# Gate projections by seven products: sums of weights formed a group ahead, in blocks of their own, and the first two gates by plain products

## The chip, the cores and the metric

One core of one Trainium2 chip. The metric is the device time of one execution in microseconds (us): the kernel before took 1498.84 us in the median of 3 runs (1498.33 to 1502.33).

## What is computed

One layer of a hybrid attention block on x of 256 rows by 2048 columns, in fp32, with 256 rows of memory:

```python
proj = rms_norm(x, g_mix) @ w_in          # heads' q, k, v and, last, 3 x 2048 gate columns
o_fox, o_sb, o_mem = ...                  # forgetting, stick-breaking and memory attention
g = sigmoid(gates.reshape(b, s, 3, 2048) + b_gate)
merged = g[..., 0, :] * (o_fox @ w_br_fox) + g[..., 1, :] * (o_sb @ w_br_sb) + g[..., 2, :] * (o_mem @ w_br_mem)
x = x + merged @ w_out
u = causal_depthwise_conv(rms_norm(x, g_ffn) @ w_up, conv_w, conv_b)
x = x + (silu(u_gate) * u_val) @ w_down
```

The change is in the gate columns of `proj`: six pieces of 1024 columns, for m = 0, 1 (the halves of the 2048 columns) and b = 0, 1, 2 (the three branches). They are called gate (m, b) here.

## The kernel before

**Splitting.** Each fp32 product is made of three faster ones. A weight tile `raw` is copied to a rounded high half `hi` by ScalarE (L141, or L278 in `parts`), and VectorE subtracts to get the low half `lo` (L142, L279). `three` (L282) issues x_hi w_hi, x_lo w_hi and x_hi w_lo, L284 to L286. There are four raw buffers of 1024 columns (`WBUFS`) and four each of `hi` and `lo` (`SBUFS`), used in turn: a split waits until TensorE is done with the piece four back.

**Old products.** `product` (L156) makes 512 columns for both halves of the rows (t = 0, 1) in two PSUM banks, from pieces of two k-tiles by 512 columns, 12 matmuls of 512 columns each, with a tick() after each piece. `proj` (L701) is `product` on `w_in`.

**Blocked products.** `blocked` (L322) makes 1024 columns by a plan, a string of groups, each for one pair of k-tiles. In a group "e" (`eight`, L342) there are 8 block products, 24 matmuls, with a tick after each 12. In a group "s" there are 7, 21 matmuls, as in Strassen's scheme: `seven_here` (L389) loads the pair's two raw tiles, forms four sums of weight blocks in place in them with four VectorE instructions (L397, L398, L401, L402), and splits them again (`hi_t`, `lo_t`, on L278 and L279). Products of sums go to four more banks Y (the name yg in the profile; the plain ones are xg). After the last "s" the generator `gathered` (L951) combines the Y banks with eight VectorE instructions and one copy, and when the gate is done four instructions on L982 add the X banks, scaled by `rstd`. `blocked` ends with finish(). PSUM has eight banks: X takes four, Y four, and before the first "s" the other four go to attention heads.

**Order of the work.** Matmuls of `three` stand in TensorE's queue in the order of the program from the gate stage on (`ordered[0]`). Small work is written as generators: `later()` queues one, `tick()` (L102) advances up to two of them (`WINDOW`) and the background ones, and `finish()` (L123) runs all that is queued to its end, with no gate matmul between. Other instructions are ordered by a scheduler by priority, within their dependencies.

**Heads.** `sb_head` (L864) is such a generator, for six stick-breaking heads, two at a time: scores z (L871, L872), exponentials and logarithms on ScalarE, masks on GpSimd (L859), suffix sums r (L888, L890) from `ls` (L883, L884), then `weighted` (L712) with L716 and L717 for the output. Heads 0 and 1 end and heads 2 and 3 run during gate (0,0); heads 4 and 5 begin in it and end in its finish().

**Preloads.** `weight_sums` (L243) is a background generator: from the first products on it loads halves of rows of w_out and w_down for later "s" groups, sums them with three VectorE instructions (L265 to L267) and stores the sums to DRAM (L270). It starts one half every 4 ticks, and every 8 ticks once `"heads"` has been issued (L983).

**Gate loop.** L942 to L986: plans in `g_plans` (L226), biases on L949, sigmoids on L985. After the gates of one m come the branch products and the merge; `merged_T` (L916) transposes the merged rows, for m = 0 during gate (1,0).

Of the kernel before, what the change touches and what calls it, by code (L numbers as in the profile page):

```python
# [11 lines left out]
AF = mybir.ActivationFunctionType  # L12
ALU = mybir.AluOpType
# [4 lines left out]
NT = S // P  # L18
D = 2048
# [12 lines left out]
C_GATE = C_MQ + MEM_W  # L32
PIECE = 1024
# [8 lines left out]
def hybrid_block(  # L42
# [25 lines left out]
    nc = tc.nc  # L68
# [12 lines left out]
    def bank(name):  # L81
        return pp.tile([P, 512], F32, tag="bank", name=name)
# [34 lines left out]
    issued = set()  # L117
# [5 lines left out]
    def finish():  # L123
        while waiting or active:
            tick(beside=False)
# [97 lines left out]


    o_plans = ("eessesse", "eesesese")
    g_plans = (("eeeeeeee", "esesesee", "esesesee"), ("eesessee", "esesesee", "esesesee"))  # L226
    d_plans = ("ef" * 5 + "ssef" * 4 + "seeee", "efefefesssfe" + "ssse" * 2 + "ssssee")
    T1, T3, T4, T2 = range(4)
    FS2, FS4, FS3, FS1 = range(4)
    in_order = tc.keep_in_program_order  # L230
# [43 lines left out]
    def parts(src, name):  # L274
        n = src.shape[1]
        hi = wp.tile([P, PIECE], F32R, tag="hi", bufs=SBUFS, name=f"hi_{name}")
        lo = wp.tile([P, PIECE], F32R, tag="lo", bufs=SBUFS, name=f"lo_{name}")
        nc.scalar.copy(hi[:, :n], src)  # L278
        nc.vector.tensor_tensor(lo[:, :n], src, hi[:, :n].bitcast(F32), ALU.subtract)  # L279
        return [(hi[:, i : i + 512], lo[:, i : i + 512]) for i in range(0, n, 512)]  # L280
# [41 lines left out]
    def blocked(name, w, nb, n0, plan, pair, sums, raw_tile, t4_tile, gathered, ready=None, form=None, apart=None):  # L322

        wv = by_k(w)
        X = [[bank(f"x{name}{nb}_{t}_{n}") for n in range(2)] for t in range(NT)]
        Y = []
        ns = plan.count("s")

        def a_of(p, j, t):
            v = pair(p, j)  # L330
            return v[:, t * P : (t + 1) * P], v[:, S + t * P : S + (t + 1) * P]

        def f_of(p, f):
            v = sums(p, f)
            return v[:, 0], v[:, 1]

        def load(k):
            raw = raw_tile(f"raw_{name}{nb}_{k}")
            nc.sync.dma_start(raw, wv[:, k, n0 : n0 + PIECE])
            return raw  # L340

        def eight(p, first, last):  # L342
            by_bank = last and apart is not None
            w = []
            for j in range(2):
                w.append(parts(load(2 * p + j), f"{name}{nb}_{2 * p + j}"))
                if not by_bank:
                    for t in range(NT):
                        for n in range(2):
                            three(X[t][n], *a_of(p, j, t), w[j][n], first and j == 0, last and j == 1)  # L350
                tick()
            if by_bank:
                for t in range(NT):
                    for n in range(2):
                        m = 256 if (t, n) == (1, 1) else 512
                        for j in range(2):
                            wj = [part[:, :m] for part in w[j][n]]
                            three(X[t][n][:, :m], *a_of(p, j, t), wj, last=j == 1)
                        if m < 512:
                            apart.append(bank("apart")[:, m:])  # L360
                            for j in range(2):
                                wj = [part[:, m:] for part in w[j][n]]
                                three(apart[0], *a_of(p, j, t), wj, j == 0, j == 1)

        def seven(p, first, last):
            kept = sums_of[name, nb, p]
            raw0 = raw_tile(f"raw_{name}{nb}_{2 * p}")
            nc.sync.dma_start(raw0[:, :512], wv[:, 2 * p, n0 : n0 + 512])
            nc.sync.dma_start(raw0[:, 512:], kept[:, T3])
# [12 lines left out]
            T1w, T2w = parts(raw2, f"t_{name}{nb}_{p}")  # L382
            three(Y[2], *f_of(p, FS1), T1w, first, last)
            three(Y[1], *f_of(p, FS2), T2w, first, last)
            (T4w,) = parts(raw3, f"t4_{name}{nb}_{p}")
            three(X[1][0], *a_of(p, 1, 1), T4w)
            tick()

        def seven_here(p, first, last):  # L389
            raw0, raw1 = load(2 * p), load(2 * p + 1)  # L390
            (B00,) = parts(raw0[:, :512], f"{name}{nb}_{2 * p}")
            three(Y[0], *a_of(p, 0, 0), B00, first, last)
            B10, B11 = parts(raw1, f"{name}{nb}_{2 * p + 1}")
            three(X[0][0], *a_of(p, 1, 0), B10)
            three(X[0][1], *f_of(p, FS4), B11)
            b0, b1 = (raw.rearrange("p (n c) -> p n c", n=2) for raw in (raw0, raw1))
            nc.vector.tensor_tensor(b0[:, 0], b0[:, 0], b0[:, 1], ALU.add)  # L397
            nc.vector.tensor_tensor(b0[:, 1], b0[:, 1], b1[:, 1], ALU.add)  # L398
# [3 lines left out]
            nc.vector.tensor_tensor(b1[:, 0], b1[:, 0], b1[:, 1], ALU.add)  # L402
# [7 lines left out]
        by_seven = seven if t4_tile else seven_here  # L410
# [145 lines left out]
    def block(name, dt=F32):  # L556
        return bp.tile([P, 1024], dt, tag="blk", name=name)
# [4 lines left out]
    def rows_of(b):  # L562
        return b.rearrange("p (t n) -> p t n", t=NT)
# [377 lines left out]
    for m in range(2):  # L941
        gate = []  # L942
        for b, plan in enumerate(g_plans[m]):
            g, bias = [], []

            def biases(m=m, b=b, bias=bias):
                for n in (2 * m, 2 * m + 1):
                    bias.append(gp.tile([P, 512], F32, tag="bg", name=f"bg_{n}_{b}"))
                    nc.sync.dma_start(bias[-1], b_gate[0, b, n * 512 : (n + 1) * 512].partition_broadcast(P))  # L949
# [21 lines left out]
            if "s" not in plan:  # L971
                biases()
            X = blocked(
                "g", w_in, f"{m}{b}", C_GATE + b * D + m * PIECE, plan, lambda p, j: xT(2 * p + j),
                lambda p, f: xs[:, p, f], raw_g, None, gathered, biases,
            )
            for n in range(2):
                if "s" not in plan:
                    g.append(rows_of(block(f"g_{m}_{b}_{n}")))
                for t in range(NT):  # L980
                    add = g[n][:, t] if "s" in plan else bias[n]
                    nc.vector.scalar_tensor_tensor(g[n][:, t], X[t][n], rstd[:, t : t + 1], add, ALU.mult, ALU.add)  # L982
            issued.add("heads")  # L983
            for n in range(2):
                sigmoid = nc.scalar.activation(g[n], g[n], AF.Sigmoid)  # L985
                if (m, b) == (0, 0):  # L986
                    in_order(sigmoid)
            gate.append(g)
        if m == 1:
            later(merged_sums())  # L990
        for n in range(2):
# [236 lines left out]
```

## Time and profile before

| | us |
|---|---|
| median of 3 runs | 1498.84 |
| the profiled execution's own time | 1498.03 |
| its span | 1496.3 |
| TensorE busy | 1470.8 |
| VectorE busy | 1211.8 |
| ScalarE busy | 843.1 |

PE is TensorE's matmuls, PEld its weight loads, DVE is VectorE, ACT ScalarE, POOL GpSimd, SP the queue that issues DMAs. A group's row reads: line, engine, operation, written<-read by the program's names without numbers, shapes, xcount, then busy us and mean ns of one, then the idle time of that engine just before and what ended it. A row of the waits reads: who waited <- for whom: us in total, times, longest. A row of the timeline reads: start, length, engine, line, what, and in brackets the idle time before and its releaser. The gates' matmuls run from 311.56 to 361.58 us (gate (0,0)), from 374.60 to 462.4 (gates (0,1) and (0,2)) and from 508.16 to 647.7 (m = 1); branch products lie between and behind.

### The profile page before, as it was taken

The numbers are of one execution on the slowest core, as the hardware profiler recorded it, in microseconds if no ns is written. First come the engines' busy times: TensorE is split into PE (matmuls) and PEld (weight loads), VectorE is DVE, ScalarE is ACT, GpSimd is POOL, SyncE is SP. The second block draws the span as 40 slices with busy tenths as digits, with TensorE's granted clock in tenths as the row PEclk, the third lists the DMA queues.
The fourth block names the chain that finished last, engine by engine and source line by source line (L and its number), as shares of the span: only waits on it lengthen the run. The fifth ranks groups of instructions, "written<-read, shape, count | busy, mean of one in ns | idle before, by whom it ended". The sixth has DMA issues, their size and how long they took to land.

```text
span 1496.3 us, 20704 instructions
## 1 busy us (share of the span) xinstructions
PE 1470.8 (98%) x7328; PEld 1232.8 (82%) x7328; DVE 1211.8 (81%) x1844; ACT 843.1 (56%) x1201; POOL 18.3 (1%) x46
## 2 busy tenths in 40 slices
PE   9999999998999999999999999999999999999999
PEld 7888888886877876788888888888888888888887
DVE  5777677876898898998887988887787777998877
ACT  6754454464554445545657665655565565675664
POOL 0000000021000000000000000000000000000000
PEclk9999999998999999999999999999999999999999
DMA  9697798786678677697867888887666666798896
GB/s 315 199 299 228 236 298 255 223 259 221 201 234 270 212 230 236 217 315 245 285 206 242 293 277 281 292 283 241 191 187 197 185 183 203 237 322 270 259 329 222
DMA packets 201430, 369.42 MB, mean 247 GB/s; under 512 B 13530, under 2 KB 82030, under 8 KB 201070
## 3 DMA queue, kind: packets, MB, share of 16 engines
q1 hardware_dynamic: 199998, 365.99, 76.4%
q10 hardware_dynamic: 1328, 2.11, 0.4%
q8 instruction: 57, 0.93, 0.3%
q14 instruction: 47, 0.39, 0.1%
HBM read 335.54 MB, written 32.51 MB: 246 GB/s over the span
## 4 chain that ended last, share of the span: by engine, by line
PE 83%; DVE 8%; DMA 5%; issue 2%; ACT 2%; POOL 0%; SPq 0%; ACTq 0%; DVEq 0%; POOLq 0%
PE u L1131 22%; PE u L1132 11%; PE xd L284 4%; PE xd L286 4%; PE xd L285 4%; DMA raw_g<-in_w_in_dram 2%; PE f L284 2%; PE f L286 2%; PE f L285 2%; PE b L286 2%; PE xg L286 2%; PE xg L284 2%; PE xg L285 2%; PE b L284 2%; PE b L285 2%
## 5 line engine op out<-in xcount | busy, mean ns | idle before, releaser
L1131 PE MATMUL u<-hT,hi_u 128*128 128x512 f32 x1232 | 428.5, 394 | 0.0
L1132 PE MATMUL u<-hT,lo_u 128*128 128x256 f32 x1232 | 341.4, 277 | 0.0
L142 DVE TENSOR_TENSOR lo_u<-raw_u,hi_u 128x1024 fp32r<-128x1024 f32 x176 | 215.0, 1222 | 83.2 <-ACT hi_u L141 82.5
L1131 PEld LDWEIGHTS u<-hT,hi_u 128*128 128x128 f32 x1232 | 231.0, 187 | 53.4
L141 ACT CAST hi_u<-raw_u 128x1024 fp32r<-128x1024 f32 x176 | 184.7, 1050 | 136.7 <-PE u L1131 117.4
L1132 PEld LDWEIGHTS u<-hT,lo_u 128*128 128x128 f32 x1232 | 231.4, 188 | 0.0
L278 ACT CAST hi_g<-raw_g 128x1024 fp32r<-128x1024 f32 (+1 forms) x96 | 92.7, 982 | 75.4 <-DMA raw_g<-in_w_in_dram 45.9
L279 DVE TENSOR_TENSOR lo_d<-raw_d,hi_d 128x1024 fp32r<-128x1024 f32 x88 | 106.7, 1222 | 20.5 <-ACT hi_d L278 17.8
L278 ACT CAST hi_d<-raw_d 128x1024 fp32r<-128x1024 f32 x88 | 92.0, 1054 | 47.8 <-PE xd L285 22.1
L279 DVE TENSOR_TENSOR lo_g<-raw_g,hi_g 128x1024 fp32r<-128x1024 f32 (+1 forms) x96 | 108.2, 1139 | 12.5 <-ACT hi_g L278 12.2
L286 PE MATMUL xg<-lo_g,xT 128*128 128x512 f32 x231 | 90.4, 391 | 1.1 <-DVE lo_g L279 1.1
L284 PE MATMUL xg<-hi_g,xT 128*128 128x512 f32 x231 | 90.9, 394 | 0.0
L285 PE MATMUL xg<-hi_g,xT 128*128 128x512 f32 x231 | 90.0, 390 | 0.0
L141 ACT CAST hi_f<-raw_f 128x1024 fp32r<-128x1024 f32 (+1 forms) x40 | 38.6, 968 | 51.7 <-PE f L285 43.1
L284 PE MATMUL xd<-hi_d,aT 128*128 128x512 f32 x170 | 66.1, 389 | 0.0
L285 PE MATMUL xd<-hi_d,aT 128*128 128x512 f32 x170 | 66.1, 389 | 0.0
L286 PE MATMUL xd<-lo_d,aT 128*128 128x512 f32 x170 | 66.1, 389 | 0.0
L1131 PE MATMUL u<-hT_rest,hi_u 128*128 128x512 f32 x176 | 62.1, 393 | 0.0
L141 ACT CAST hi_s<-raw_s 128x1024 fp32r<-128x1024 f32 (+1 forms) x40 | 38.4, 961 | 40.9 <-PE s L285 25.7
L1103 ACT ACTIVATE y<-u,taps 128x256 f32<-128x256 f32 x88 | 49.2, 595 | 14.7 <-DVE u L1100 14.7
L142 DVE TENSOR_TENSOR lo_f<-raw_f,hi_f 128x1024 fp32r<-128x1024 f32 (+1 forms) x40 | 44.4, 1117 | 15.2 <-ACT hi_f L141 13.5
L142 DVE TENSOR_TENSOR lo_s<-raw_s,hi_s 128x1024 fp32r<-128x1024 f32 (+1 forms) x40 | 44.4, 1115 | 14.8 <-ACT hi_s L141 14.4
(467 smaller groups left out, 3323.2 us busy)
## 6 DMA issues: line engine op xcount, KB each, us to landing
raw_u<-in_w_up_dram SPq DMA_DIRECT2D x176, 512.0 KB, 4.6
raw_g<-in_w_in_dram SPq DMA_DIRECT2D x96, 512.0 KB, 4.4
raw_d<-in_w_down_dram SPq DMA_DIRECT2D x66, 512.0 KB, 5.3
pre_d<-in_w_down_dram SPq DMA_DIRECT2D x88, 256.0 KB, 4.7
kept_d<-pre_d SPq DMA_DIRECT2D x44, 512.0 KB, 5.9
raw_f<-in_w_in_dram SPq DMA_DIRECT2D x32, 512.0 KB, 5.0
raw_s<-in_w_in_dram SPq DMA_DIRECT2D x32, 512.0 KB, 5.3
raw_o<-in_w_out_dram SPq DMA_DIRECT2D x25, 512.0 KB, 5.4
```

The costliest lines, as they stand in the source:

```text
L141: pin(nc.scalar.copy(hi[:, :m], raw[:, :m]))
L142: pin(nc.vector.tensor_tensor(lo[:, :m], raw[:, :m], hi[:, :m].bitcast(F32), ALU.subtract))
L278: nc.scalar.copy(hi[:, :n], src)
L279: nc.vector.tensor_tensor(lo[:, :n], src, hi[:, :n].bitcast(F32), ALU.subtract)
L284: fix(nc.tensor.matmul(o, lhsT=ah, rhs=w[0], start=first, stop=False))
L285: fix(nc.tensor.matmul(o, lhsT=al, rhs=w[0], start=False, stop=False))
L286: fix(nc.tensor.matmul(o, lhsT=ah, rhs=w[1], start=False, stop=last))
L1103: nc.scalar.activation(y, u[:, 2:], AF.Identity, scale=tap(2), bias=tap(3))
L1131: nc.tensor.matmul(ps[i], lhsT=hi[:, j, c], rhs=hT(k + j), start=first, stop=False)
L1132: nc.tensor.matmul(ps[i][:, :S], lhsT=lo[:, j, c], rhs=hT(k + j)[:, :S], start=False, stop=last)
```

## The change

Gates (0,0) and (0,1) get empty plans: they are made by `proj` in two halves each, and their sums are scaled with the bias added. The plan of gate (1,0) becomes that of the others. So 12 groups by seven are left of 15. In the gates' groups "s" the sums go to two tiles of the pool `block`, `t13` and `t42` (t0_g and t1_g in the program's names); a new function `prepared` issues the loads and the sums directly after the group before has been issued. `ready`, which loads the biases, now also calls finish(), sets `"heads"` and applies the sigmoid of gates (0,0) and (0,1) when it is first called, at the first "s" of gate (0,2); and it is called before the Y banks are taken.

```diff
-    g_plans = (("eeeeeeee", "esesesee", "esesesee"), ("eesessee", "esesesee", "esesesee"))
+    g_plans = (("", "", "esesesee"), ("esesesee", "esesesee", "esesesee"))
...
+        def prepared(p):
+            raw0, raw1 = load(2 * p), load(2 * p + 1)
+            t13, t42 = (t4_tile(f"t{i}_{name}{nb}_{p}") for i in range(2))
+            b0, b1, u, v = (w.rearrange("p (n c) -> p n c", n=2) for w in (raw0, raw1, t13, t42))
+            nc.vector.tensor_tensor(u[:, 0], b0[:, 0], b0[:, 1], ALU.add)
+            nc.vector.tensor_tensor(u[:, 1], b0[:, 1], b1[:, 1], ALU.add)
+            nc.vector.tensor_tensor(v[:, 1], u[:, 0], b1[:, 1], ALU.add)
+            nc.vector.tensor_tensor(v[:, 0], v[:, 1], b1[:, 0], ALU.add)
+            return raw0, raw1, t13, t42
...
         def seven_here(p, first, last):
-            raw0, raw1 = load(2 * p), load(2 * p + 1)
+            raw0, raw1, t13, t42 = ahead.pop(p)
...
-            b0, b1 = (raw.rearrange("p (n c) -> p n c", n=2) for raw in (raw0, raw1))
-            nc.vector.tensor_tensor(b0[:, 0], b0[:, 0], b0[:, 1], ALU.add)
-            nc.vector.tensor_tensor(b0[:, 1], b0[:, 1], b1[:, 1], ALU.add)
             tick()
-            T1w, T3w = parts(raw0, f"t_{name}{nb}_{2 * p}")
-            nc.vector.tensor_tensor(b1[:, 1], b1[:, 1], b0[:, 0], ALU.add)
-            nc.vector.tensor_tensor(b1[:, 0], b1[:, 0], b1[:, 1], ALU.add)
+            T1w, T3w = parts(t13, f"t_{name}{nb}_{2 * p}")
...
-            T4w, T2w = parts(raw1, f"t_{name}{nb}_{2 * p + 1}")
+            T4w, T2w = parts(t42, f"t_{name}{nb}_{2 * p + 1}")
...
                 if s == 0:
+                    if ready:
+                        ready()
                     Y += [bank(f"y{name}{nb}_{j}") for j in range(4)]
-                if s == 0 and ready:
-                    ready()
                 by_seven(s, s == 0, s == ns - 1)
...
+            if name == "g" and plan[i + 1 : i + 2] == "s":
+                ahead[s] = prepared(s)
...
+            def ready():
+                finish()
+                if "heads" not in issued:
+                    issued.add("heads")
+                    for v in gate[0] + gate[1]:
+                        in_order(nc.scalar.activation(v, v, AF.Sigmoid))
                 biases()
...
+            if not plan:
+                biases()
+                for n in range(2):
+                    ps = proj(c0 + n * 512, 512, f"g{n}_{b}")
+                    g.append(rows_of(block(f"g_{m}_{b}_{n}")))
+                    scaled_sums(n, ps, [bias[n]] * NT)
+                continue
```

In the changed kernel the four sums are on lines L393 to L396.

More of the change, by code (lines that the diff above doesn't have):

```diff
@@ L408, in seven_here @@
             tick()
-        by_seven = seven if t4_tile else seven_here
+        by_seven = seven_here if name == "g" else seven
+        ahead = {}
         s, e = 0, ns
@@ L969, in gathered, with scaled_sums @@
                 scaled(g[1][:, 1], f, rneg[:, 1:2], 1)
-            if "s" not in plan:
-                biases()
+            def ready():
[4 more added lines that the diff above has]
+                        in_order(nc.scalar.activation(v, v, AF.Sigmoid))
+                biases()
+            def scaled_sums(n, ps, add):
+                for t in range(NT):
+                    nc.vector.scalar_tensor_tensor(g[n][:, t], ps[t], rstd[:, t : t + 1], add[t], ALU.mult, ALU.add)
+            c0 = C_GATE + b * D + m * PIECE
+            gate.append(g)
+            if not plan:
[5 more added lines that the diff above has]
+                continue
             X = blocked(
-                "g", w_in, f"{m}{b}", C_GATE + b * D + m * PIECE, plan, lambda p, j: xT(2 * p + j),
-                lambda p, f: xs[:, p, f], raw_g, None, gathered, biases,
+                "g", w_in, f"{m}{b}", c0, plan, lambda p, j: xT(2 * p + j), lambda p, f: xs[:, p, f], raw_g, block,
+                gathered, ready,
             )
             for n in range(2):
[L978 to L988, printed above, removed]
+                scaled_sums(n, [X[t][n] for t in range(NT)], [g[n][:, t] for t in range(NT)])
+                nc.scalar.activation(g[n], g[n], AF.Sigmoid)
         if m == 1:
```

## The prediction

> **What bounds the kernel now.** I read the page first, then the table of busy time by stretches, then the order of TensorE's instructions where that table shows a hole, and last the waits of the stretches that the change touches.
>
> ```profile
> PE 1470.8 (98%) x7328; PEld 1232.8 (82%) x7328; DVE 1211.8 (81%) x1844; ACT 843.1 (56%) x1201; POOL 18.3 (1%) x46
> PEclk9999999998999999999999999999999999999999
> PE 83%; DVE 8%; DMA 5%; issue 2%; ACT 2%; POOL 0%; SPq 0%; ACTq 0%; DVEq 0%; POOLq 0%
> ```
>
> TensorE is the bound: it is busy for 98% of the span and holds 83% of the chain that ended last. So time is won only where TensorE stands still or runs slowly, and lost by every matmul added. The one slice of the granted clock below 9 lies in the tenth slice, 337 to 374 us, inside the gate stage.
>
> ```profile
> core 0: us, PE busy (x) PEld busy (x) DVE busy (x) ACT busy (x) POOL busy (x), PEclk, DMA share, GB/s
> 311.50:361.60 50.10, 50.10 (x235) 41.95 (x233) 31.06 (x45) 25.60 (x39) 5.76 (x12) 1.00 0.79 259
> 361.60:374.60 13.00, 5.79 (x19) 4.04 (x17) 10.37 (x18) 3.85 (x7) 4.06 (x8) 0.62 0.44 137
> 374.60:462.40 87.80, 85.47 (x368) 68.20 (x368) 77.92 (x95) 47.29 (x51) 0.00 (x0) 1.00 0.70 230
> 508.16:647.70 139.54, 131.67 (x558) 102.31 (x557) 124.87 (x156) 69.14 (x75) 0.00 (x0) 1.00 0.70 228
> ```
>
> The stretches are: gate (0,0), all "e"; a hole of 13.0 us at a granted clock of 0.62; gates (0,1) and (0,2); the three gates of m = 1. To see what each should take I need the pace of a matmul when nothing waits:
>
> ```profile
> 337.27 0.39 PE L286 MATMUL xg<-lo_g,xT 128*128 128x512 f32 x1
> ...
> 338.63 0.40 PE L286 MATMUL xg<-lo_g,xT 128*128 128x512 f32 x1
> 338.86 0.53 PE L888 MATMUL r<-ls,after_r 128*128 128x384 f32 x2
> ...
> 339.96 0.45 PE L284 MATMUL xg<-hi_g,xT 128*128 128x512 f32 x1
> ...
> 348.21 0.59 PE L716 MATMUL z<-sb,vs 128*128 128x256 f32 x2
> ...
> 349.43 0.48 PE L284 MATMUL xg<-hi_g,xT 128*128 128x512 f32 x1
> ```
>
> From 337.27 to 338.63 six matmuls start, 0.227 us each (the 0.39 of a row is its pipelined length). An "e" group is 24 matmuls, 5.45 us; an "s" group 21, 4.77 us. The same rows give a reference for a pair of stick-breaking heads: sums "r" 339.96 - 338.86 = 1.10 us, products "z" 349.43 - 348.21 = 1.22 us.
>
> By this pace gates (0,1) and (0,2), 2 x 183 matmuls by the plans, need 366 x 0.227 = 83.1 us and took 87.8: **4.7 lost**. The three of m = 1 need 549 x 0.227 = 124.6 and took 139.5: **14.9 lost**, a little of it the eight transposes of the merge, which stay. The hole:
>
> ```profile
> 361.58 0.39 PE L286 MATMUL xg<-lo_g,xT_rest 128*128 128x512 f32 x1
> 363.67 0.44 PE L888 MATMUL r<-ls,after_r 128*128 128x384 f32 x1 [1.70 <-ACT ls L883]
> ...
> 372.02 1.22 PE L716 MATMUL z<-sb,vs 128*128 128x256 f32 x2 [5.04 <-POOL sb L859]
> ...
> 374.60 0.61 PE L284 MATMUL xg<-hi_g,xT 128*128 128x512 f32 x1
> ```
>
> Heads 4 and 5 end here with no gate matmul between their steps, because the gate's call ends with finish(): 13.0 us for 1.10 + 1.22 = 2.3 us of work, **10.7 lost**. The idle is 1.70 + 5.04 us and short ones; the rest is the low clock (the four z take 374.60 - 372.02 = 2.58 us against 1.22). The budget is 10.7 + 4.7 + 14.9 = 30.3 us.
>
> What TensorE waits for in the groups by seven:
>
> ```profile
> ACT hi_t_g L278 <- DVE raw_g L398: 15.1, 7, 4.2
> ACT hi_t_g L278 <- DVE raw_g L402: 14.6, 7, 3.4
> ...
> PE yg L286 <- DVE lo_t_g L279: 3.0, 5, 0.7
> PE xg L284 <- ACT hi_t_g L278: 2.2, 4, 0.8
> PE xg L286 <- DVE lo_t_g L279: 2.1, 4, 0.5
> PE yg L284 <- ACT hi_t_g L278: 1.4, 3, 0.9
> ```
>
> All four name the halves hi_t and lo_t of the sums. The chain is: VectorE forms a sum in place (L397 to L402), ScalarE copies its high half, VectorE subtracts the low half, TensorE starts. The sums stand in VectorE's order among and behind the group's own splits, so the chain is run while TensorE is already in the group. The gate loads are no cause: ScalarE waits for them, but ends early.
>
> **The change, part by part.** Times are sums against the profiled execution's own 1498.03 us, of which 1496.3 is the span; the median of the three runs shown is 0.8 higher.
>
> *Three groups by seven become "e"* (15 to 12): 3 x 3 = 9 matmuls more, 9 x 0.227 = **+2.0**. All on the path, as TensorE has no slack.
>
> *Gates (0,0) and (0,1) by the older product()*: each is two halves of eight pieces, one tick per piece of 12 matmuls, the same matmuls and ticks as "e". No finish() stands between them. By the built order heads 4 and 5 get the spacing that heads 2 and 3 have today: 60 gate matmuls between scores and r, then 36 before the closing z; today it is 36 and then none. Heads 2 and 3 did r and z in 1.10 and 1.22 us with no wait, so the hole goes down to that: **-10.4**, leaving 0.3 for a late semaphore. What is late next is VectorE, and there it has room: gate (0,0) used 31.06 of 50.1 us, the heads' work and three preloads included. A half and the one after it hold four banks and two heads the other four, so no gate matmul waits for a head's bank.
>
> The loads of product() are two runs of 512 columns instead of one of 1024:
>
> ```profile
> raw_g<-in_w_in_dram SPq DMA_DIRECT2D x96, 512.0 KB, 4.4
> ...
> raw_s<-in_w_in_dram SPq DMA_DIRECT2D x32, 512.0 KB, 5.3
> ```
>
> raw_s is the same form: 0.9 us later. [...] Four buffers at 12 x 0.227 = 2.7 us a piece are 10.9 us of lead, so I take 0.
>
> *"heads" is issued one gate later*, so the preloads of w_down keep their shorter period for it: two more halves early (SP, VectorE), two fewer later. Each costs VectorE about 1.5 us by the next rows; gate (0,1) no longer forms sums and hides them: 0.
>
> *Four sigmoids in one place (ready(), first "s" of gate (0,2)) instead of two and two*. Queued behind them on ScalarE are the high halves of that group, and TensorE waits for those.
>
> ```profile
> L985 ACT ACTIVATE g<-g 128x1024 f32<-128x1024 f32 x10 | 10.3, 1055 | 1.0 <-DVE g L982 0.9
> L985 ACT ACT_TABLE_LOAD x1 | 1.3, 1283 | 0.0
> ```
>
> In the built order the table load and three sigmoids, 1.3 + 3 x 1.06 = 4.5 us, precede the group's first high half, and the fourth stands between its second and third. The high half before them can run 5.4 us before the gate's first matmul ends its predecessor, and the "e" group covers 5.45 more, so 4.5 + 1.1 is hidden: 0; 5.6 if that cover were gone.
>
> *Sums in blocks of their own, formed ahead.* The work stays: the rows are
>
> ```profile
> L279 DVE TENSOR_TENSOR lo_g<-raw_g,hi_g 128x1024 fp32r<-128x1024 f32 x62 | 75.2, 1220 | 5.8 <-ACT hi_g L278 5.6
> L279 DVE TENSOR_TENSOR lo_t_g<-raw_g,hi_t_g 128x1024 fp32r<-128x1024 f32 x30 | 36.6, 1221 | 11.2 <-ACT hi_t_g L278 9.4 <-PE yg L285 1.4
> ...
> L982 DVE SCALAR_TENSOR_TENSOR g<-xg,rstd,g 128x512 f32<-128x512 f32 x18 | 12.6, 743 | 0.0
> ...
> L402 DVE TENSOR_TENSOR raw_g<-raw_g 128x512 f32<-128x512 f32 x15 | 10.3, 690 | 0.4
> ...
> L265 DVE TENSOR_TENSOR pre_d<-pre_d 128x512 f32<-128x512 f32 x12 | 8.2, 684 | 0.0
> ```
>
> What moves is the order: three of the four sums now stand between the splits of the "e" before and the group's first split, the fourth behind that split; so the chain through ScalarE is two splits ahead of TensorE's need. The block is released by the splits themselves, and the raw buffer comes free once its own split and sums are done instead of after the split of the sums, one to two splits (1.2 to 2.4 us) earlier. So the 11.2 us that VectorE idles ahead of lo_t should mostly go.
>
> But VectorE is nearly full: 124.87 us in three gates is 41.6 a gate, and TensorE needs 183 x 0.227 = 41.5. What remains is therefore bounded by nothing lost and today's 19.6. From "s" to "s" across a gate border VectorE must do six splits of "e" groups (6 x 1.22), the gather and closing ops (eight of some 0.72, four of 0.74), three ops of a preload (0.68 and two half as wide, 1.5) and three first sums (2.1), 19.6 us less the overlap of some 0.07 per op, 18.0; TensorE takes 3 x 5.45 = 16.4 there. The four buffers of each half make up about 1 us of the rest: I take 1.5 us lost at each of the two such borders (into gates (1,1) and (1,2)), 0.3 in each of the 12 groups and 0.7 for the transposes: 3.0 + 3.6 + 0.7 = 7.3 instead of 19.6, **-12.3**. I stay off the lower end because the engine that must keep up has no more than a few tenths of slack a gate.
>
> *ready() before the Y banks, with finish() in it*, puts the merge's transposes after 24 matmuls instead of 36 in gate (1,0). They need the second merge sum, which VectorE ends some 2.3 us into that 5.45 us group: 0.
>
> Sum: +2.0 - 10.4 - 12.3 = -20.7; 1498.03 - 20.7 = 1477.3, and 0.8 up to the median: **1478**.
>
> **Rivals.**
> *A. VectorE sets the pace of the gates by seven.* Then order helps nothing: those gates keep their 19.6 lost, and only the hole goes: 1498.8 + 2.0 - 10.4 = 1490.4, say 1490. For it: 41.6 against 41.5 us a gate. Against it: VectorE itself stood still for 139.5 - 124.9 = 14.7 us in these gates, so it was kept, not keeping. [...]
>
> *B. The heads' hole comes back in another place*, in the finish() of ready(): 1498.8 + 2.0 - 12.3 = 1488.5. The built order speaks against it: the last z stands ahead of the middle of gate (0,1). This is also the case in which that part doesn't do what it says.
>
> *C. Slower: a sum at the head of VectorE's queue waits for its load.* Ahead of time means that L393 stands before splits that TensorE needs; if the raw tile isn't there, those wait too.
>
> ```profile
> DMA to landing us min/median/max: 3.4/4.4/6.2
> ```
>
> The load is issued when the same buffer's last split ends, five splits and a sum ahead of its use, about 6.3 us; today's slowest landing is 6.2. If landings grow beyond 6.3 by 3 us, every group loses 3: 12 x 3 = 36 in place of 19.6, and 1490.4 + 36 - 19.6 = 1506.8, say 1507. It ends above 1498.8 as soon as a group loses (19.6 + 8.4) / 12 = 2.3 us. The DMA share of 0.70 in these gates speaks against it.
>
> **How the numbers follow.** Forecast 0.72, A 0.13, B 0.07, C 0.08. The best case is that all 30.3 go but the nine matmuls, 1498.8 - 28.3 = 1470.5. The forecast's own range is 1471 to 1486; A and B lie above, so the range is 1471 to 1491, which leaves out C and a little of the rest. About 0.3% (4.5 us) is what this measurement can tell from no change; faster than 1494.3 are the forecast, A and B but for a part of A: 0.88; within, 0.05; slower, 0.07.
>
> **What would show it.** Right: no TensorE wait on POOL L859 and no dip of the granted clock in gate (0,1); the r and z of heads 4 and 5 in 1.1 and 1.2 us; gates of m = 1 in 129 to 132 us with VectorE busy over 94% of it; waits of ScalarE on the sums gone. Wrong: TensorE waiting for hi_t or lo_t as often as now (A); VectorE idle at L393 behind raw_g (C); ScalarE late by the four sigmoids at the first "s" of gate (0,2).

## The result and the profile after

The changed kernel took 1474.65 us in the median of 4 runs (1473.68 to 1475.67), the kernel before 1499.59 beside it (4 runs, 1498.33 to 1502.33): a ratio of 0.9831, 95% interval 0.9814 to 0.9848. The forecast was 1478, with a range of 1471 to 1491. The profiled execution took 1474.81 us, its span is 1473.1 (before 1498.03 and 1496.3).

The page of the changed kernel: busy time of the engines, the granted clock in 40 slices, and the shares of the chain that ended last.

```profile
PE 1462.5 (99%) x7337; PEld 1234.5 (84%) x7337; DVE 1190.8 (81%) x1818; ACT 838.6 (57%) x1194; POOL 17.1 (1%) x46
PEclk9999999999999999999999999999999999999999
PE 93%; DMA 3%; DVE 2%; ACT 1%; issue 1%; SPq 0%; POOL 0%; DVEq 0%; ACTq 0%; POOLq 0%
```

There are nine more matmuls (7337 for 7328), and yet TensorE is busy for 8.3 us less: busy time counts a row's whole length (0.39 us at a pace of 0.227), so each wait that breaks the overlap of rows adds to it (the row behind the wait of 1.61 us at 420.75 us is 0.50 long), and so does a low clock (a row of two z matmuls of 256 columns that is 0.59 us long now was 1.22 in the hole of before, at a clock of 0.62). The dip in the tenth slice is gone, and TensorE now holds 93% of the chain, where it held 83%. Next the table of stretches: gates (0,0) and (0,1), gate (0,2), the three gates of m = 1.

```profile
core 0: us, PE busy (x) PEld busy (x) DVE busy (x) ACT busy (x) POOL busy (x), PEclk, DMA share, GB/s
313.23:409.40 96.17, 96.17 (x442) 80.36 (x442) 64.76 (x89) 47.99 (x65) 8.66 (x20) 1.00 0.83 267
409.54:453.20 43.66, 42.05 (x184) 34.13 (x183) 40.43 (x52) 24.55 (x26) 0.00 (x0) 1.00 0.82 271
497.79:624.99 127.20, 126.84 (x558) 103.74 (x557) 121.75 (x155) 70.96 (x76) 0.00 (x0) 1.00 0.79 253
```

The gates of m = 1 went from 139.54 to 127.20 us, for 124.6 us of matmuls at the pace of 0.227. VectorE is busy for 121.75 / 127.20 = 96% of that, as against 89% before, with 3 us less of it in a stretch that is 12 us shorter. The DMA share rose from 0.70 to 0.79. Heads 4 and 5, in TensorE's order:

```profile
368.91 0.53 PE L896 MATMUL r<-ls,after_r 128*128 128x384 f32 x2
...
370.02 0.45 PE L284 MATMUL g<-hi_g,xT 128*128 128x512 f32 x1
...
378.26 0.59 PE L724 MATMUL z<-sb,vs 128*128 128x256 f32 x2
...
379.49 0.48 PE L284 MATMUL g<-hi_g,xT 128*128 128x512 f32 x1
```

The sums r take 370.02 - 368.91 = 1.11 us, the products z 379.49 - 378.26 = 1.23, with gate matmuls between them and no wait: what heads 2 and 3 took before. All that TensorE waits for from 313 to 625 us is three rows:

```profile
PE xg L286 <- DVE lo_t_g L279: 1.6, 1, 1.6
PE xg L286 <- DVE lo_g L279: 0.4, 2, 0.2
PE r L896 <- DVE ls L892: 0.2, 1, 0.2
```

**Where the time came from.** I count the gate stage from its first matmul to the first one of the product with w_out (xo): 311.56 to 692.73 us before, 313.23 to 669.48 after, 381.2 and 356.2 us. That is 24.9 less; the stage begins 1.7 later, behind work that no edit touches, and 24.9 - 1.7 is the span's 23.2. By stretches (before, after): the three gates of m = 0 151.05 and 140.08; the branch products of m = 0 45.55 and 44.48; the gates of m = 1 139.57 and 127.20; the branch products of m = 1 about 0.5 less.

### The profile page after: what moved, and what is told of

Its sections match the earlier page's. It is cut to its first block, busy times and chain, and to the rows that moved or that the text cites. A ratio compares the mean times of both kernels' runs of the same rounds, so it can differ in the third digit from the quotient of the medians.

```text
span 1473.1 us, 20668 instructions
## 1 busy us (share of the span) xinstructions
PE 1462.5 (99%) x7337; PEld 1234.5 (84%) x7337; DVE 1190.8 (81%) x1818; ACT 838.6 (57%) x1194; POOL 17.1 (1%) x46
## 4 chain that ended last, share of the span: by engine, by line
PE 93%; DMA 3%; DVE 2%; ACT 1%; issue 1%; SPq 0%; POOL 0%; DVEq 0%; ACTq 0%; POOLq 0%
PE u L1149 22%; PE u L1150 11%; PE xd L286 4%; PE xd L285 4%; PE xd L284 4%; PE xg L286 3%; PE xg L285 3%; PE xg L284 3%; PE f L286 2%; PE f L285 2%; PE f L284 2%; PE b L286 2%; PE b L284 2%; PE b L285 2%; PE g L284 2%; PE g L286 2%
## 5 line engine op out<-in xcount | busy, mean ns | idle before, releaser
L278 ACT CAST hi_g<-raw_g 128x1024 fp32r<-128x1024 f32 (+1 forms) x64 | 62.1, 972 | 38.3 <-DMA raw_g<-in_w_in_dram 9.5
L279 DVE TENSOR_TENSOR lo_g<-raw_g,hi_g 128x1024 fp32r<-128x1024 f32 (+1 forms) x64 | 71.2, 1117 | 0.0
L141 ACT CAST hi_b<-raw_b 128x1024 fp32r<-128x1024 f32 x32 | 33.7, 1052 | 42.8 <-PE b L285 17.8
L142 DVE TENSOR_TENSOR lo_s<-raw_s,hi_s 128x1024 fp32r<-128x1024 f32 (+1 forms) x40 | 44.4, 1115 | 14.9 <-ACT hi_s L141 14.6
L286 PE MATMUL xg<-lo_g,xT 128*128 128x512 f32 x140 | 54.8, 391 | 0.4 <-DVE lo_g L279 0.4
L284 PE MATMUL xg<-hi_g,xT 128*128 128x512 f32 x140 | 54.5, 389 | 0.0
```

The source lines that it names most:

```text
L141: pin(nc.scalar.copy(hi[:, :m], raw[:, :m]))
L142: pin(nc.vector.tensor_tensor(lo[:, :m], raw[:, :m], hi[:, :m].bitcast(F32), ALU.subtract))
L284: fix(nc.tensor.matmul(o, lhsT=ah, rhs=w[0], start=first, stop=False))
L286: fix(nc.tensor.matmul(o, lhsT=ah, rhs=w[1], start=False, stop=last))
```

## The experiments

Each run's time stands beside runs of the kernel before on the same chip (1500.37 us beside e1 to e4, 1500.99 beside e5 to e8, 1499.98 beside e9 to e12). The changed kernel was timed beside 1499.59 alone, so a difference of an experiment against its 1474.65 is uncertain by the 1.4 us between these four. As the start of the stage moves by up to 4 us between kernels that are the same up to there (309.5 to 313.8), the stage's length in the trace tells more of where the time lies than the total. It is that of one execution, though, and profiled executions lie up to 3.4 us from their kernel's median (e9: 1490.61 against 1487.2). All kernels are the changed one but for the edit shown, and e3 has the gate loop of before as well.

| kernel | median (range), us | ratio, 95% | stage, us | gates (1,0), (1,1), (1,2), us |
|---|---|---|---|---|
| before | 1499.59 (1498.33 to 1502.33) | 1 | 381.2 | 46.6, 47.3, 45.6 |
| after | 1474.65 (1473.68 to 1475.67) | 0.9814 to 0.9848 | 356.2 | 42.7, 42.2, 42.3 |
| e1_sums_in_old_place | 1476.57 (1475.54 to 1477.72) | 0.9826 to 0.9856 | 360.5 | 45.0, 42.3, 42.1 |
| e2_sums_in_place | 1487.33 (1485.8 to 1489.1) | 0.9895 to 0.9928 | 371.4 | 42.7, 46.1, 46.4 |
| e3_sums_ahead_only | 1484.74 (1483.32 to 1489.16) | 0.988 to 0.9915 | 368.0 | 46.6, 42.9, 42.3 |
| e4_gate01_by_seven | 1480.78 (1478.72 to 1482.11) | 0.985 to 0.9883 | 365.1 | 42.7, 42.3, 42.3 |
| e5_eight_with_finish | 1484.33 (1481.95 to 1485.05) | 0.987 to 0.9899 | 367.6 | 42.7, 42.3, 42.3 |
| e6_eight_no_finish | 1476.15 (1474.53 to 1478.7) | 0.9822 to 0.9852 | 361.5 | 42.7, 42.3, 42.3 |
| e7_one_more_add | 1473.21 (1471.09 to 1476.27) | 0.9801 to 0.9834 | 356.3 | 42.7, 42.9, 43.2 |
| e8_splits_in_order | 1489.29 (1485.48 to 1490.28) | 0.9906 to 0.9933 | 373.0 | 51.1, 44.7, 45.4 |
| e9_in_place_more_buffers | 1487.2 (1485.22 to 1490.61) | 0.9901 to 0.9928 | 372.4 | 48.8, 42.7, 42.4 |
| e10_raw_held | 1488.53 (1486.8 to 1489.24) | 0.9905 to 0.9929 | 369.7 | 42.7, 46.9, 48.9 |
| e11_sums_in_order | 1473.26 (1469.46 to 1476.87) | 0.98 to 0.9835 | 357.1 | 42.7, 42.3, 42.3 |
| e12_three_more_adds | 1500.1 (1496.29 to 1502.64) | 0.9988 to 1.0009 | 381.7 | 46.2, 49.7, 49.7 |

183 matmuls at 0.227 us are 41.5 us a gate, the floor of the last column.

### The two halves of the change

**e2_sums_in_place**: the gates by plain products stay, the sums go back into the raw tiles, where and when the kernel before made them.

```diff
-            raw0, raw1, t13, t42 = ahead.pop(p)
+            raw0, raw1 = load(2 * p), load(2 * p + 1)
...
-            T1w, T3w = parts(t13, f"t_{name}{nb}_{2 * p}")
+            T1w, T3w = parts(raw0, f"t_{name}{nb}_{2 * p}")
...
-            if name == "g" and plan[i + 1 : i + 2] == "s":
-                ahead[s] = prepared(s)
```

> The changed kernel with seven_here as it was before (sums in place, in their old place); products for gates (0,0) and (0,1), 12 groups. Theory: only the heads' hole and the nine matmuls are left of the change, and the gates of m = 1 take 138 to 140 us: 1474.7 + 12.4 + 2.3 = 1489, against 1499.6 before. Rival (VectorE's load set the pace, and three groups fewer are what relieved it): 1475 to 1480.

**e3_sums_ahead_only**: the sums in blocks of their own and ahead, the plans and the gate loop of before.

```diff
-    g_plans = (("", "", "esesesee"), ("esesesee", "esesesee", "esesesee"))
+    g_plans = (("eeeeeeee", "esesesee", "esesesee"), ("eesessee", "esesesee", "esesesee"))
```

> The kernel before with the sums ahead in blocks of their own, and nothing else of the change: 15 groups, gate (0,0) by eight, finish() at its end. Theory (the two halves of the change add up): the hole of 13 us stays, the gates of m = 1 take 127 to 129 us, nine matmuls fewer than in the changed kernel: 1474.7 + 10.7 - 2.0 + 1 = 1484. Rival (the sums ahead need the idle VectorE that the two plain gates leave): 1490 or more.

The totals came where the theory had them. The stage is 9.8 us shorter by the first half alone (381.2 - 371.4; forecast -10.4 + 2.0 = -8.4) and 13.2 by the second alone (forecast -12.3); together 23.0, and the whole change has 24.9. So the two nearly add up, and each pays for itself.

The gates of m = 1 did not come as expected: 135.2 us in e2 for 138 to 140, and 131.8 in e3 for 127 to 129. Both misses lie mostly in gate (1,0), the one gate of m = 1 whose plan changes, from "eesessee" to "esesesee". It takes 46.6 us in the kernel before and in e3, which have the old plan, and 42.7 in e2, which has the new plan with the sums in place and late. All four waits of TensorE in gate (1,0) of the kernel before lie in the third "s" (the gate's matmuls 115 to 135), which the old plan puts directly behind the second:

```profile
538.60 0.51 PE L284 MATMUL yg<-hi_t_g,xs 128*128 128x512 f32 x1 [0.92 <-ACT hi_t_g L278]
...
539.87 0.50 PE L286 MATMUL yg<-lo_t_g,xs 128*128 128x512 f32 x1 [0.53 <-DVE lo_t_g L279]
...
541.60 0.50 PE L284 MATMUL xg<-hi_t_g,xT 128*128 128x512 f32 x1 [0.54 <-ACT hi_t_g L278]
...
542.86 0.49 PE L286 MATMUL xg<-lo_t_g,xT 128*128 128x512 f32 x1 [0.53 <-DVE lo_t_g L279]
```

So about 3.9 us of the gain in m = 1 seem to go with the plan, and not with blocks or order. That is read from traces and not shown by an experiment: no run changes this plan alone, e2 also has the new ready(), and in e3 some 2 us of the loss lie at the first "s".

### What made the groups by seven faster

**e1_sums_in_old_place**: blocks of their own as in the change, but the four sums stand where they stood before, inside the group.

```diff
         def prepared(p):
...
-            nc.vector.tensor_tensor(u[:, 0], b0[:, 0], b0[:, 1], ALU.add)
...
         def seven_here(p, first, last):
...
+            nc.vector.tensor_tensor(u[:, 0], b0[:, 0], b0[:, 1], ALU.add)
+            nc.vector.tensor_tensor(u[:, 1], b0[:, 1], b1[:, 1], ALU.add)
             tick()
             T1w, T3w = parts(t13, f"t_{name}{nb}_{2 * p}")
+            nc.vector.tensor_tensor(v[:, 1], u[:, 0], b1[:, 1], ALU.add)
+            nc.vector.tensor_tensor(v[:, 0], v[:, 1], b1[:, 0], ALU.add)
```

> The changed kernel, but the four sums stand where they stood before, behind the first splits of their own group; they still go to blocks of their own. Theory (what helps is that the sums stand ahead in VectorE's order): the waits for hi_t and lo_t return, the three gates of m = 1 take 136 to 140 us instead of 127.2, gate (0,2) about 3 us more than now; in all 1484 to 1490. Rival (what helps is that the raw buffers come free earlier, since the sums no longer lie in them): the gates stay at 127 to 130 us, 1475 to 1478.

Here my theory fell. Without any order ahead the kernel kept nearly all: 1476.57 us, 1.9 over the changed kernel's 1474.65, with intervals that overlap (in the traces the stage is 4.3 us longer, and 2.3 of it are in gate (1,0)). Against e2, with the sums in the same place and only the tile another, it is 10.8 us faster; of 10.9 in the traces 8.1 lie in gates (1,1) and (1,2). Gate (1,0) goes the other way, by 2.3 us: ScalarE there stands 5.05 us for the transposes of the merge ahead of the first high half of the sums, where in the changed kernel these copies follow it. ScalarE's waits in the gates of m = 1 tell why the other two are faster. The kernel before:

```profile
ACT hi_g L278 <- DMA raw_g<-in_w_in_dram: 28.6, 17, 3.6
ACT hi_t_g L278 <- DVE raw_g L398: 13.1, 6, 4.2
ACT hi_t_g L278 <- DVE raw_g L402: 11.3, 5, 3.4
```

e2:

```profile
ACT hi_g L278 <- DMA raw_g<-in_w_in_dram: 30.6, 19, 2.4
ACT hi_t_g L278 <- DVE raw_g L408: 12.1, 5, 3.9
```

e1:

```profile
ACT hi_t_g L278 <- DVE t_g L404: 25.1, 9, 3.4
ACT hi_g L278 <- DMA raw_g<-in_w_in_dram: 7.7, 7, 2.9
```

The changed kernel:

```profile
ACT hi_g L278 <- DMA raw_g<-in_w_in_dram: 6.0, 4, 1.8
```

In e1 the waits for the sums are as long as before (25.1 us in 9 for 24.4 in 11), and cost nearly nothing: gates (1,1) and (1,2) take 42.3 and 42.1 us. What went are the waits for loads, from 28.6 in the kernel before and 30.6 in e2 to 7.7 us. I read it so: ScalarE can wait for a sum and still be in time as long as its queue has run ahead of TensorE, and loads that come late take that lead away. What the loads' issue waits for in the gates of m = 1, before and after:

```profile
SPq L339 <- DVE lo_t_g L279: 49.4, 15, 6.9
```

```profile
SPq L339 <- DVE lo_g L279: 73.8, 35, 5.6
```

SP waits for a raw buffer in both kernels. Before, it waits longest for splits of the sums (lo_t); in the changed kernel that row is gone, and it waits for plain splits alone but for some 6 us.

**e10_raw_held**: everything as changed, sums ahead and in blocks of their own, but two instructions of one column keep each raw tile in use until the sums are split, as it was when they were made in it. The column written is one that has been split already.

```diff
             T1w, T3w = parts(t13, f"t_{name}{nb}_{2 * p}")
+            nc.vector.tensor_tensor(t13[:, :1], t13[:, :1], raw0[:, :1], ALU.add)
...
             T4w, T2w = parts(t42, f"t_{name}{nb}_{2 * p + 1}")
+            nc.vector.tensor_tensor(t42[:, :1], t42[:, :1], raw1[:, :1], ALU.add)
```

> The changed kernel, sums ahead in blocks of their own, with one VectorE instruction of one column behind each split of the sums that reads the raw tile once more, so that the raw buffers come free as late as before the change (the column is written to the block of the sums, whose content has been used by then). New theory (buffers): the waits on the load return, 1483 to 1489. Rival (order ahead): 1475 to 1478, the price of the 24 small instructions alone.

1488.53 us: the total is back where e2 was (1487.33), by 24 instructions of 156 ns each, 3.7 us in all. The loss lies in gates (1,1) and (1,2), 46.9 and 48.9 us; gate (1,0) keeps its 42.7. SP's own waits in the gates of m = 1, then ScalarE's and VectorE's:

```profile
SPq L339 <- DVE t_g L408: 58.9, 9, 9.0
```

```profile
ACT hi_g L278 <- DMA raw_g<-in_w_in_dram: 41.5, 21, 4.1
DVE t_g L394 <- DMA raw_g<-in_w_in_dram: 7.2, 4, 2.2
```

SP stands at the load of L339 for up to 9.0 us until the small instruction on L408 has let a raw buffer go. So the loads come late, and ScalarE waits 41.5 us for them. The sums stand ahead as in the changed kernel, and that saves nothing. It can add to the loss: the sums now wait for the late loads themselves (7.2 us at L394), with splits behind them in VectorE's queue, which is rival C's mechanism.

**e9_in_place_more_buffers**: the reverse: sums in place and late as in e2, but the pair's raw tiles come from the pool `block`, so that they hold none of the four raw buffers.

```diff
-            raw0, raw1, t13, t42 = ahead.pop(p)
+            raw0, raw1 = (t4_tile(f"raw_{name}{nb}_{2 * p + j}") for j in range(2))
+            for j, raw in enumerate((raw0, raw1)):
+                nc.sync.dma_start(raw, wv[:, 2 * p + j, n0 : n0 + PIECE])
```

> As e2 (sums in place and in their old place, two plain gates, 12 groups), but the raw tiles of the groups by seven are loaded into blocks, so that the four raw buffers serve the groups e alone. The new theory, after e1 (the load of the next raw tile waited for a buffer that the sums held until their splits were done): the waits on the load go although the sums are still in place and late: 1475 to 1479. Rival (sums in place are slow since they must wait for the splits of the same data): 1485 to 1488, as e2.

The total, 1487.2, came out as the rival said, but not in the way it said. Gates (1,1) and (1,2) take 42.7 and 42.4 us, with the sums in place and late: within 0.5 us of the changed kernel's. So that sums in place must wait for splits of the same data, the rival's reason, costs these gates nothing. What is lost lies at the first "s" of gates (0,2) and (1,0). TensorE's order in gate (0,2), the only waits from 409 to 424 us:

```profile
413.29 0.51 PE L286 MATMUL xg<-lo_g,xT 128*128 128x512 f32 x1 [0.18 <-DVE lo_g L279]
421.48 0.80 PE L284 MATMUL yg<-hi_g,xT 128*128 128x512 f32 x1 [5.59 <-ACT hi_g L278]
```

SP's queue, just ahead of it:

```profile
407.17 6.43 SPq L339 DMA_DIRECT2D raw_g<-in_w_in_dram  x4
413.65 0.90 SPq L402 DMA_DIRECT2D raw_g<-in_w_in_dram  x2
```

The load into the block is issued behind four loads that wait for raw buffers, and lands too late once. In gate (1,0) it is not a load: ScalarE stands for the transposes of the merge, with the first high halves of the "s" behind them.

```profile
513.00 1.07 ACT L175 CAST mT<-mt 128x512 fp32r<-128x512 f32 x2 [10.49 <-PE mt L937]
```

So e9 bears the buffers out in gates (1,1) and (1,2), and its total can't be used for that: the edit moved the first load of a gate and the order on ScalarE as well. A version without these moves wasn't tried.

### The hole of heads 4 and 5

**e4_gate01_by_seven**: gate (0,1) gets its three groups by seven back.

```diff
-    g_plans = (("", "", "esesesee"), ("esesesee", "esesesee", "esesesee"))
+    g_plans = (("", "esesesee", "esesesee"), ("esesesee", "esesesee", "esesesee"))
```

> The changed kernel with gate (0,1) by seven again, so that finish() in ready() comes 24 matmuls into that gate. The built order then has 60 matmuls ahead of r of heads 4 and 5 but none between r and the closing z. Theory: the wait before r is gone and that before z stays, about 7 us with the low clock, less 2.0 for nine matmuls fewer, 1 more for three more groups: 1474.7 + 7 - 2 + 1 = 1480.7. Rival (the 24 matmuls cover it): 1473 to 1474, a better kernel.

**e5_eight_with_finish** and **e6_eight_no_finish**: gates (0,0) and (0,1) as eight groups "e" in one call each, with the same number of matmuls as the change has; in e5 the call ends with finish(), in e6 it doesn't.

```diff
-    g_plans = (("", "", "esesesee"), ("esesesee", "esesesee", "esesesee"))
+    g_plans = (("eeeeeeee", "eeeeeeee", "esesesee"), ("esesesee", "esesesee", "esesesee"))
...
-                    ps = proj(c0 + n * 512, 512, f"g{n}_{b}")
```

```diff
-        finish()
+        if name != "g" or "s" in plan:
+            finish()
```

> The changed kernel, but gates (0,0) and (0,1) are made by blocked() with eight groups e each, four banks at a time, and finish() at each end as before; no products by halves. Theory (finish() makes the hole): the hole of 13 us is back behind gate (0,0), 1474.7 + 10.7 = 1485. Rival (something else in the old gates, such as loads or preloads): 1475 to 1478.

> As e5, but finish() is left out at the end of gates (0,0) and (0,1), so that the steps of heads 4 and 5 have 60 and 36 matmuls between them again. The four banks of gate (0,1) can then only be had when the four of gate (0,0) are scaled, as the heads hold the others. Theory (finish() alone makes the hole, banks cost a little): 1475 to 1478, with a wait of at most 3 us at the border. Rival (banks are what makes the hole, and halves of two banks are what cures it): 1482 to 1486.

All three totals came as the theory had them. In e4 the finish() of ready() stands before gate (0,1)'s first "s", and the closing z waits there:

```profile
375.78 1.22 PE L724 MATMUL z<-sb,vs 128*128 128x256 f32 x2 [7.12 <-POOL sb L867]
```

In e5 the hole is that of the kernel before, between the two gates:

```profile
363.74 0.44 PE L896 MATMUL r<-ls,after_r 128*128 128x384 f32 x1 [1.62 <-ACT ls L891]
...
371.31 1.22 PE L724 MATMUL z<-sb,vs 128*128 128x256 f32 x2 [3.38 <-POOL sb L867]
...
374.20 1.22 PE L724 MATMUL z<-sb,vs 128*128 128x256 f32 x2 [1.25 <-POOL sb L867]
...
375.50 0.77 PE L284 MATMUL xg<-hi_g,xT 128*128 128x512 f32 x1
```

Taking only finish() away (e6) is worth 1484.33 - 1476.15 = 8.2 us. That e6 isn't quite the changed kernel has another reason: a gate of 1024 columns needs the four X banks that the gate before has yet to close. In the profiled execution, at 1478.7 us the slowest of e6's four, the stage is 5.3 us longer, and TensorE waits once, for 4.03 us where I expected 3 at most:

```profile
367.68 0.79 PE L284 MATMUL xg<-hi_g,xT 128*128 128x512 f32 x1 [4.03 <-DVE g L990]
```

and VectorE, whose queue holds those closing instructions, stood before them at a preload's first sum, behind its load:

```profile
360.63 0.69 DVE L265 TENSOR_TENSOR pre_d<-pre_d 128x512 f32<-128x512 f32 x1 [4.67 <-DMA pre_d<-in_w_down_dram]
...
366.88 2.72 DVE L990 SCALAR_TENSOR_TENSOR g<-xg,rstd,bg 128x512 f32<-128x512 f32 x4
```

The halves of product() need only two banks at a time, which is why the change has no such border.

### How full VectorE is

**e7_one_more_add** and **e12_three_more_adds**: one and three sums of 512 columns more in each group by seven, into a block that the last sum overwrites.

```diff
             nc.vector.tensor_tensor(v[:, 1], u[:, 0], b1[:, 1], ALU.add)
+            nc.vector.tensor_tensor(v[:, 0], b0[:, 0], b1[:, 1], ALU.add)
```

> The changed kernel with one more VectorE instruction of 128x512 in each of the 12 groups by seven (its result is overwritten), 0.61 to 0.69 us each, 7.8 us in all. Theory (after the change VectorE is just short of setting the pace, 121.8 us busy of 127.2 in the gates of m = 1): part of it shows, 1476 to 1479. Rival A (VectorE sets the pace): all of it, 1482. Rival (VectorE has room): 1475.

> The changed kernel with three more VectorE instructions of 128x512 in each group by seven (results overwritten), 3 x 0.61 to 0.69 us in each of 12 groups, 23 us in all and 17.5 us in the gates of m = 1. One more cost nothing (e7). Theory (VectorE idles 5.5 us in the 127.2 us of these gates after the change, so it now has to set the pace): the gates of m = 1 take 12 us more, gate (0,2) 3 more, 1488 to 1492. Rival (the idle counted is not the room there is): 1476 to 1482.

The first adds 12 x 0.69 = 8.3 us of instructions to VectorE and costs nothing that can be measured in the total: 1473.21, where my theory had 1476 to 1479. The second adds 36 x 0.69 = 25 us and costs 25.5, more than my theory's 1488 to 1492. The gates of m = 1, in e7 and in e12:

```profile
492.48:621.24 128.76, 127.21 (x559) 103.53 (x557) 126.64 (x163) 70.97 (x76) 0.00 (x0) 1.00 0.75 249
```

```profile
503.13:648.77 145.64, 133.85 (x559) 101.67 (x557) 137.47 (x180) 67.79 (x73) 0.00 (x0) 1.00 0.71 220
```

In e7 VectorE is busy for 98% of the stretch, and gates (1,1) and (1,2) are already 0.6 and 0.9 us longer in the trace, for 3 x 0.69 = 2.1 us of work each. In e12 they take 7.4 us more than in the changed kernel for 3 x 3 x 0.69 = 6.2 us of work: all of it shows, and more. So the room of a gate is less than about 2 us. Why three sums cost more than their length was not taken apart; VectorE is busy for 94% of that stretch (137.47 / 145.64), so that it alone sets the pace there isn't shown.

### The order on VectorE

**e8_splits_in_order**: sums and splits on VectorE in the order of the program. **e11_sums_in_order**: the sums alone.

```diff
-        nc.vector.tensor_tensor(lo[:, :n], src, hi[:, :n].bitcast(F32), ALU.subtract)
+        fix = in_order if ordered[0] else lambda ins: ins
+        fix(nc.vector.tensor_tensor(lo[:, :n], src, hi[:, :n].bitcast(F32), ALU.subtract))
```

```diff
-            nc.vector.tensor_tensor(u[:, 0], b0[:, 0], b0[:, 1], ALU.add)
+            in_order(nc.vector.tensor_tensor(u[:, 0], b0[:, 0], b0[:, 1], ALU.add))
```

(the same for the other three sums, and both edits in e8)

> The changed kernel with the sums and the splits of the gates and later blocked products kept in the program's order on VectorE, so that the first sum of a group no longer stands before the last split of the group before, as it does once, in gate (0,2), where TensorE waits 1.6 us behind a load. Theory: that wait goes, 1473. Rival (what the scheduler moved forward was worth something elsewhere, or the gather is late instead): 1476 or more.

> The changed kernel with the four sums alone kept in the program's order on VectorE; the splits are free as in the changed kernel. By the built order the first sum of the second group of gate (0,2) then stands behind the last split of the first group. Theory (that sum, waiting for its load, is what holds TensorE 1.6 us there): 1473, the gates of m = 1 as now. Rival (as in e8, order costs more than it gives): 1477 or more.

e8 is 14.6 us worse than the changed kernel, so my theory was wrong here. Half of the loss lies in gate (1,0), 51.1 us for 42.7: TensorE waits 2.19 and 2.02 us for low halves that VectorE makes late, and the granted clock is 0.57 and 0.56 in the 3.4 us behind these waits. At each of the next two borders the four closing instructions now stand ahead of a split that TensorE needs, and wait for the last matmul into their banks. VectorE, then TensorE, at the first of them:

```profile
547.22 2.79 DVE L990 SCALAR_TENSOR_TENSOR g<-xg,rstd,g 128x512 f32<-128x512 f32 x4 [0.82 <-PE xg L287]
549.92 1.22 DVE L280 TENSOR_TENSOR lo_g<-raw_g,hi_g 128x1024 fp32r<-128x1024 f32 x1
```

```profile
551.19 0.50 PE L287 MATMUL xg<-lo_g,xT 128*128 128x512 f32 x1 [1.52 <-DVE lo_g L280]
```

e11 was to take away the one long wait that the changed kernel has left. VectorE in gate (0,2) of the changed kernel:

```profile
418.87 0.69 DVE L393 TENSOR_TENSOR t_g<-raw_g 128x512 f32<-128x512 f32 x1 [1.72 <-DMA raw_g<-in_w_in_dram]
419.48 1.22 DVE L279 TENSOR_TENSOR lo_t_g<-t_g,hi_t_g 128x1024 fp32r<-128x1024 f32 x1
```

A first sum of the next group waits 1.72 us for its load, and the split behind it in the queue is the one for which TensorE waits 1.6. In e11 this wait is gone and others of up to 0.8 us stand in the same gate (44.2 us for 43.8). 1473.26 us against 1474.65 can't be told apart; no version here is shown to beat the changed kernel.

## Why the prediction was right, and where it was wrong

**The bound and the budget** were right. Of the 30.3 us that I found lost, 25.4 are gone (10.7 of the hole and 14.7 of the groups), and 2.0 went to the added matmuls. The total fell by 24.9 us for 20.7 forecast.

**The heads' hole**, forecast -10.4 with 0.3 left: -10.7, nothing left. e4, e5 and e6 bear out the cause: finish() with no gate matmuls between the heads' steps. Of rival B there is nothing in the changed kernel; e4 shows the place where it would have come, and its price in the total, 1480.78 - 1474.65 = 6.1 us though nine matmuls are fewer.

**Nine matmuls**, +2.0: the matmuls are there (7337 for 7328), at the pace of 0.227.

**What I set at 0** (the loads of product(), the preloads, the sigmoids, ready() before the banks): the three rows of waits from 313 to 625 us hold no term of these. Gates (0,0) and (0,1) take 96.17 us: 384 x 0.227 = 87.2, heads' matmuls the rest.

**The groups by seven**, forecast -12.3: the three gates of m = 1 gave 12.4 and gate (0,2) with (0,1) another 2.3, 14.7 together. The size was near, the reason wrong: it was near because the loss was counted in the trace and VectorE's load capped what I let go, and as far as the mechanism goes that was luck. The step that failed is "The gate loads are no cause: ScalarE waits for them, but ends early", and with it the sentence that gives the gain to the order, "the chain through ScalarE is two splits ahead of TensorE's need". That the raw buffer comes free one to two splits earlier I wrote down as a consequence; in gates (1,1) and (1,2) it is the main cause. e2 to e1 changes the buffers and not the sums' place: 10.8 us. e9 leaves the sums in place and frees the buffers, and these two gates are at 42.7 and 42.4 us. e10 keeps the order and holds the buffers: 13.9 us lost. e1 to the changed kernel gives the order: 1.9 us in the medians, which can't be told from nothing, 4.3 in the traces, none of it in gates (1,1) and (1,2). My sign "waits of ScalarE on the sums gone" came (24.4 us before, 3.7 after) and proves nothing, as e1 keeps these waits. I should have followed ScalarE's 28.6 us of waits for loads one step further, to what SP was waiting for: it is the raw buffer, held by sums made in it.

**The plan of gate (1,0)** had no term beyond its matmuls: I gave all of the loss in m = 1 to the chain of the sums. By the traces about 3.9 of the 12.4 us belong to this gate and seem to go with its plan, which puts no "s" directly behind another.

**What was left**: 7.3 us forecast, 4.9 measured. The 1.5 at each of two gate borders did not come; gates (1,1) and (1,2) are within 0.8 us of the floor. The changed kernel's single long wait is rival C's mechanism, once and for 1.6 us.

**Rival A** (VectorE sets the pace) is refuted by the result, 12.4 us gained in the gates of m = 1 with the same sums and splits to make, and by e7, one sum more in each group at no cost in the total; e12 shows that the room is small. A sum costs nearly what it did, 682 to 684 ns in a block of its own (L393 to L396) for 685 to 690 in place (L397 to L402), so the gain isn't one of VectorE's work.

**Not forecast**: 1.1 and 0.5 us less in the branch products, and 1.7 us lost ahead of the stage. Those of m = 0 take 44.5 us in e1 and the changed kernel and 46.8 and 47.2 in e2 and e10, where TensorE waits once, 2.05 and 2.38 us, for the low half of a branch weight; why that half is late stays open. The 1.7 us lie within what the start of the stage moves by between kernels that are the same up to there.

**What stays open**: the exact share of the order beside the buffers (1.9 to 4.3 us); what the plan of gate (1,0) is worth alone; whether e9 without its losses in gates (0,2) and (1,0) would have reached e1; why e12 lost more than its work.

## What to carry to other kernels

When an engine waits for a load, ask what the load's issue waited for: here the DMA queue stood for a buffer that was held because sums were made in it, and a tile of its own for the result was worth 10.8 us (e2 to e1). A wait that an engine shows need not be a cost: e1 kept 25 us of ScalarE's waits for sums and lost 2. Compare stage by stage, too: two halves whose totals came out as forecast hid 3.9 us that seem to belong to neither reason. To tell two such reasons apart, undo each alone: the same data in another tile, and the old holding time with one tiny instruction.

## What the runs showed that I had not expected

**The granted clock can fall after short waits.** In e1 TensorE waited 0.56 and 1.15 us around two matmuls near 416 us, and then:

```profile
416.00:417.60 1.60, 0.49 (x2) 0.05 (x1) 1.60 (x3) 1.60 (x3) 0.00 (x0) 1.00 0.71 261
417.60:421.00 3.40, 3.36 (x9) 2.66 (x10) 3.40 (x5) 1.56 (x2) 0.00 (x0) 0.55 0.41 96
```

The clock was 0.55 for 3.4 us, and the nine matmuls from 417.64 to 421.39 us took 3.75 us instead of 9 x 0.227 = 2.04: 1.7 us on top of 1.7 us of waiting. In e8 single waits of 2.19 and 2.02 us were followed by a clock of 0.57 and 0.56. But the length of the wait doesn't decide it. Two waits of 1.28 and 0.70 us in e2 and two of 1.22 and 0.59 us later in e1 itself were followed by none of this (the mean clock over the gates of m = 1, where they lie, is 1.00 in both), nor was the changed kernel's wait of 1.6 us (the matmuls behind it start 0.23 us apart), nor a single one of 2.38 us in e10, behind which the clock stayed at 1.00:

```profile
458.20:461.60 3.40, 3.40 (x15) 2.82 (x16) 3.35 (x3) 0.90 (x1) 0.00 (x0) 1.00 0.66 210
```

What decides it, these runs don't show.
